# A decoder block's gate matrix, built by one-hot matmuls or scattered into cleared DRAM

## The chip, the cores and the metric

One core of one Trainium2 chip. The metric is the device time of one execution in microseconds (us), the median of the runs. The kernel before takes 4041.68 us (three runs, 4041.59 to 4042.62).

## The reference, cut to what matters

One layer of a decoder with 512 tokens and a model width of 2048: a linear recurrence and a latent attention side by side, a channel mixer called PEER, a gated embedding and a last norm. The change is in PEER:

```python
s1 = jnp.einsum('nhc,kc->nhk', q[:, :, 0], k1)      # 8 heads, 128 keys a half
s2 = jnp.einsum('nhc,kc->nhk', q[:, :, 1], k2)
v1, i1 = lax.top_k(s1, K)                           # K = 16
v2, i2 = lax.top_k(s2, K)
cand = (v1[..., :, None] + v2[..., None, :]).reshape(N, PEER_HEADS, K * K)
cv, ci = lax.top_k(cand, K)
e_idx = i1[ci // K] * 128 + i2[ci % K]              # 16384 experts
gate = softmax(cv)
z = einsum('thkd,td->thk', u_tab[e_idx], h)
out = einsum('thk,thkd->td', gelu(z) * gate, v_tab[e_idx])
```

Each token has 8 heads x 16 = 128 slots; a slot is an expert (a pair i1, i2 of 128 values each) and a gate. The 16 experts of one head differ; two heads can choose the same expert, and then their gates add up.

## The kernel before, in words

All matmuls run on float32 numbers split into a high and a low float32r part, three products each (`mm3`, L147 to L149). Weights come in blocks of 128x2048 by `Ahead` (L121 to L144): SyncE's queue (SP) loads a block two steps ahead into four half-block buffers, ScalarE (ACT) writes the high part (L111), VectorE (DVE) the low part (L112), one step ahead of TensorE (PE).

PEER treats its tokens in two groups. For group A (the first 128 tokens) GpSimd (POOL) gathers each token's expert rows by an indirect DMA, one slot of 128 tokens each (`gather`, L777); DVE multiplies a gathered row of `peer_u` with h and sums it (`dot_u`, L783 to L790) and then issues the gather that is two slots ahead, since there are two row buffers. Group B (the other 384 tokens) takes a dense path: all experts' z are computed for all tokens and multiplied with a gate matrix G over (i1, i2, token), which is zero where a token has not chosen the expert.

The U loop (L1010) has 128 steps, one per value j of i2: 48 matmuls of 384 columns give z for 128 experts and 384 tokens; ACT applies Gelu and stores it to `z_s` in DRAM (`finish`, L982). The V loop has 128 steps too: `act_load` (L991) brings z and G of four j back on SP's queue, `act_mul` (L1000) multiplies, `act_split` splits, and 48 matmuls of 384 columns follow. The first `act_load` stands in step 122 of the U loop, the first `act_mul` in step 124.

The top-k of group B's three blocks of 128 tokens (`topk`, `prep_B`) and the gate matrix are spread over the U loop's steps by a list of work with costs (L964 to L971): block 0's top-k in steps 7 to 23; then twice 36 steps with the next block's top-k and the gate matrices of the block before (a list of 32 quads of four tokens); and in the last 22 steps, up to step 117, block 2's quads. The gate matrix of a quad is made by `gate_tokens` (L821): per token ACT makes a one-hot row of i1 (L832, L838), DVE a one-hot row of i2 times the gate's two parts (L833), PE a matmul of 256 columns (L843); ACT and DVE write the result into `stage` (L848, L849), and every 32 tokens ACT's queue sends 2 MB to `G_s` (L851). Before that, `turn` (L801) transposes i1, i2 and the gates of a block (L807, L810). A hold keeps further work back for two steps around these.

The whole stretch from L871 on is under `tc.manual_schedule()`: every engine's instructions run in the order in which they are written. Earlier, `gate_proj` (L449), 32 times, multiplies x with the columns of the two branches' gates, while attention and the merge go on; each is one block of weights.

Of the kernel before, what the change touches and what calls it, by code (L numbers as in the profile page):

```python
# [10 lines left out]
F32 = mybir.dt.float32  # L11
F32R = mybir.dt.float32r
U32 = mybir.dt.uint32
# [20 lines left out]
def _pieces(value, count, bits):  # L34
    """value as a sum of `count` float32 numbers; all but the last have `bits` significant bits."""
    out, rest = [], value
    for _ in range(count - 1):
        m, e = math.frexp(rest)
        p = math.ldexp(math.floor(m * 2 ** bits), e - bits)
        out.append(p)  # L40
        rest -= p
    out.append(float(np.float32(rest)))
    return out
# [3 lines left out]
def kernel(ctx: ExitStack, tc: tile.TileContext, a, dbg=None):  # L47
# [14 lines left out]
    # ---------------------------------------------------------------- helpers  # L62
# [14 lines left out]
    class Ring:  # L77
        """Buffers taken in turn."""
# [14 lines left out]
    class Stream:  # L93
        """A [128, 2048] block of weights, loaded and split in two halves: part(i, n) is the i-th of n
        pieces as two float32r parts whose sum is exact."""
# [25 lines left out]
    class Ahead:  # L121
        """Streams of a list of blocks: loaded two steps ahead, split one step ahead."""
# [28 lines left out]
    def split(hi, lo, src, gain=None):  # L151
        """hi + lo = src * gain, both float32r."""
        if gain is None:
            S.activation(hi, src, AF.Copy)
            V.tensor_tensor(lo, src, hi.bitcast(F32), op=OP.subtract)  # L155
        else:
            S.activation(hi, src, AF.Copy, scale=gain)
            V.scalar_tensor_tensor(lo, src, gain, hi.bitcast(F32), op0=OP.mult, op1=OP.subtract)

    def cols_proj(src, xh, xl, kt=KT):  # L160
        """PSUM [128 output columns, T] for one column tile."""
# [6 lines left out]
    def rows_proj(srcs, blocks, before=None):  # L168
        """PSUM [128 tokens, 512 columns] for each token block."""
# [12 lines left out]
    def rstd_cols(ss, n, name):  # L182
        """[128 tokens, blocks] of 1/sqrt(ss/n + eps)."""
# [13 lines left out]
    def sums_over_features(sq):  # L197
        """[128 tokens, 4] PSUM sums over the partitions of sq [128, T]."""
# [6 lines left out]
    def rows_of(rc, out=None):  # L205
        """[128, tokens], in out or else in PSUM: every partition holds the row of rc."""
# [11 lines left out]
    class SumSq:  # L218
        """Sum of squares of [128, T] chunks over features."""
# [18 lines left out]
    # ---------------------------------------------------------------- constants  # L238
    masks = const.tile([128, 384], F32R, name="masks")
    cst = const.tile([128, 386], F32, name="cst")  # L240
    negmask, ident, iota = cst[:, :128], cst[:, 128:256], cst[:, 256:384]
    freq, sgn = cst[:, 384:385], cst[:, 385:386]
    tril = const.tile([128, 128], U32, name="tril")
# [16 lines left out]
    # ---------------------------------------------------------------- DRAM scratch  # L260
# [8 lines left out]
    G_s = dram.tile([NB // TC, 128, 128 * TC], F32, name="G_s")  # L269

    # ---------------------------------------------------------------- x * gain, split
# [28 lines left out]
    # ---------------------------------------------------------------- HGRN2  # L300
# [147 lines left out]
    # ---------------------------------------------------------------- gates (kept before the sigmoid)  # L448
    def gate_proj(src, dst):  # L449
        ps = cols_proj(src, xh, xl)  # L450
        t = t2()
        V.tensor_tensor(t, ps, rr_mix, op=OP.mult)
        nc.sync.dma_start(dst, t)

    # ---------------------------------------------------------------- MLA
# [17 lines left out]
    # rotary tables: angle = position * frequency, reduced to [-pi, pi]  # L473
# [49 lines left out]
    for hp in range(4):  # L523
# [21 lines left out]
        # a head's rotary part: its 64 rows of high parts, and in the other 64 rows their low parts  # L545
# [58 lines left out]
    # ---------------------------------------------------------------- merge  # L604
# [33 lines left out]
    opool.release()  # L638

    # ---------------------------------------------------------------- residual, second norm  # L640
# [45 lines left out]
    # ---------------------------------------------------------------- PEER top-k  # L686
    def topk16(*rows):
        """The 16 largest of each row (values, indices, row); the rows are overwritten."""
# [12 lines left out]
    def topk(b, i1o, i2o, gate):  # L701
        """Steps (cost, function) that fill i1o, i2o, gate: [128 tokens, 8 heads * 16] float32."""
# [57 lines left out]
    # ---- group A: expert rows gathered for the first 128 tokens  # L760
# [31 lines left out]
    # ---- group B: the gate matrix [i1, i2, token]  # L792
    slots = {}
    after_pe, after_pe_next, hold = [], [], [0]

    def prep_B(b):
        i1 = upool.tile([128, 128], F32, name="i1", bufs=2)
        i2 = upool.tile([128, 128], F32, name="i2", bufs=2)
        gt = upool.tile([128, 128], F32, name="gt", bufs=1)

        def turn():  # L801
            slots[b] = upool.tile([128, 4, 128], F32, name="slots", bufs=1)

            def pe():
                ps = mx()
                for n, t in enumerate((i1, i2, gt)):
                    TE.transpose(ps[:, n * 128:n * 128 + 128], t, ident)  # L807

                def act():
                    S.activation(flat(slots[b][:, :2]), ps[:, :256], AF.Copy)  # L810
                    split(slots[b][:, 2].bitcast(F32R), slots[b][:, 3], ps[:, 256:384])
                return act

            after_pe.append(lambda: after_pe_next.append(pe))
            hold[0] = 2

        return topk(b + 1, i1, i2, gt) + [(0, turn)]

    stage = [None]

    def gate_tokens(t0):  # L821
        """Gate matrices of tokens t0 .. t0+3 of group B."""
        if t0 % TC == 0:
            stage[0] = upool.tile([128, 128, TC], F32, name="stage", bufs=1)
        st = stage[0]
        hot = []
        for i in range(4):
            b, t = divmod(t0 + i, 128)
            l = upool.tile([128, 128], F32R, name="ohl", bufs=8)
            r = upool.tile([128, 2, 128], F32R, name="ohr", bufs=8)  # L830
            i1T, i2T = (slots[b][:, n, t:t + 1] for n in range(2))
            S.activation(l, iota, AF.Abs, scale=-1.0, bias=i1T)  # L832
            V.scalar_tensor_tensor(r, iota[:, None, :].to_broadcast([128, 2, 128]), i2T,  # L833
                                   slots[b][:, 2:4, t:t + 1].to_broadcast([128, 2, 128]),
                                   op0=OP.is_equal, op1=OP.mult)
            hot.append((l, r))
        for l, _ in hot:
            S.activation(l, l.bitcast(F32), AF.Relu, scale=-1.0, bias=ones[:, :1])  # L838

        def pe():  # L840
            ps = wide()
            for i, (l, r) in enumerate(hot):
                TE.matmul(ps[:, i * 256:i * 256 + 256], lhsT=l, rhs=flat(r), start=True, stop=True)  # L843

            def act():
                o = t0 % TC
                hi, lo = (ps.rearrange("p (t s j) -> p s j t", t=4, s=2)[:, n] for n in range(2))
                S.activation(st[:, :, o:o + 4], hi, AF.Copy)  # L848
                V.tensor_tensor(st[:, :, o:o + 4], st[:, :, o:o + 4], lo, op=OP.add)  # L849
                if o == TC - 4:  # L850
                    nc.scalar.dma_start(G_s[t0 // TC], flat(st))  # L851
            return act

        after_pe.append(pe)
        if t0 % TC == TC - 4:
            hold[0] = 2

    def merge(*lists):
        """The lists' steps in one list, each list spread evenly over it."""
# [3 lines left out]
    quads = [[(2, lambda t=t: gate_tokens(t)) for t in range(b * 128, (b + 1) * 128, 4)] for b in range(3)]  # L863

    def phase(steps, work):
        """The work with costs that sum to the steps of the loop it takes."""
# [3 lines left out]
    # ---------------------------------------------------------------- PEER scores  # L870
    ordered = tc.manual_schedule()  # L871
# [37 lines left out]
    def rows_of_h(c):  # L909
        """Group A's h by rows, 512 of its columns."""  # L910
# [10 lines left out]
    for cg in range(4):  # L921
# [28 lines left out]
        if cg == 0:  # L950
# [11 lines left out]
            # the top-k steps of group A that need the heads of a column group only  # L962
# [5 lines left out]
            for b in (1, 2):  # L968
                prep = prep_B(b)
                work += phase(MIX, merge(prep[:-1], quads[b - 1]) + prep[-1:])  # L970
# [20 lines left out]
    def act_load(grp, q):  # L991
# [3 lines left out]
        o = (grp * NJ + q * NQ) * TC  # L995
        nc.sync.dma_start(gt.rearrange("p t j i -> p t (j i)"),
                          G_s.rearrange("t p x -> p t x")[:, :, o:o + NQ * TC])
        parts_in[grp, q] = (zt, gt)

    def act_mul(grp, j):  # L1000
        zt, gt = parts_in[grp, j // NQ]
        zj = zt[:, j % NQ].rearrange("p (t i) -> p t i", i=TC)
        V.tensor_tensor(zj, zj, gt[:, :, j % NQ], op=OP.mult)
# [6 lines left out]
    for j in range(NU):  # L1010
# [6 lines left out]
        if j >= NF:  # L1017
            n = j + 1 - NF
            hold[0] = max(0, hold[0] - 1)
            while work and spent < n and not hold[0] and len(after_pe) < 2:  # L1020
# [13 lines left out]
        todo = after_pe + after_pe_next  # L1034
        after_pe.clear()
        after_pe_next.clear()
        for f in todo:
            g = f()
            if g:
                late.append(g)  # L1040
        if j == NU - 7:
            for f in late[1:]:
                f()
            late = late[:1]
# [4 lines left out]
            gts = Ring(vwA, 2, [128, NB // TC, 4, TC], F32, "gt")  # L1049
# [326 lines left out]
```

## Time and profile before

| what | value |
|---|---|
| median of three runs | 4041.68 us |
| the profiled execution: span from the first to the last instruction | 4040.0 us |
| what the profile shows around the span | nothing; the median is 1.7 us longer |
| PE busy | 4005.3 us (99%) |
| DVE busy | 2621.1 us (65%) |
| ACT busy | 1597.2 us (40%) |
| POOL busy | 347.6 us (9%) |
| DMA | 862.68 MB, mean 214 GB/s |
| granted TensorE clock | 0.998 |

The page gives busy times per engine and, in 40 slices of the span, each engine's busy tenths. A busy PE is not PE at its peak, since matmuls overlap: their starts, not their durations, give their pace. POOL's spans are rough. An idle engine that is not the bottleneck costs nothing.

### The profile page before, as it was taken

The numbers are of one execution on the slowest core, as the hardware profiler recorded it, in microseconds if no ns is written. First come the engines' busy times: TensorE is split into PE (matmuls) and PEld (weight loads), VectorE is DVE, ScalarE is ACT, GpSimd is POOL, SyncE is SP. The second block draws the span as 40 slices with busy tenths as digits, with TensorE's granted clock in tenths as the row PEclk, the third lists the DMA queues.
The fourth block names the chain that finished last, engine by engine and source line by source line (L and its number), as shares of the span: only waits on it lengthen the run. The fifth ranks groups of instructions, "written<-read, shape, count | busy, mean of one in ns | idle before, by whom it ended". The sixth has DMA issues, their size and how long they took to land. (4 is left out here: it accounts for less than half of the span.)

```text
span 4040.0 us, 54629 instructions
## 1 busy us (share of the span) xinstructions
PE 4005.3 (99%) x21191; PEld 3667.2 (91%) x21191; DVE 2621.1 (65%) x3992; ACT 1597.2 (40%) x2582; POOL 347.6 (9%) x262
## 2 busy tenths in 40 slices
PE   9999999999999999999999999999999999999998
PEld 7878777778888889999999999999999999999976
DVE  5352554443343343699998998977777888877744
ACT  5342433332332242325566555753333333333443
POOL 0000000000000000021221211111111111111000
PEclk9999999999999999999999999999999999999999
DMA  5222222334444442478787788789888888888432
GB/s 210 97 74 94 72 96 84 102 105 141 151 141 133 141 140 99 166 286 304 283 303 283 287 302 298 293 332 356 317 297 315 312 311 312 299 313 310 169 117 97
DMA packets 264515, 862.68 MB, mean 214 GB/s; under 512 B 24128, under 2 KB 94272, under 8 KB 229568
## 3 DMA queue, kind: packets, MB, share of 16 engines
q1 hardware_dynamic: 202064, 531.57, 38.5%
q0 software_dynamic: 36864, 268.45, 17.8%
q10 hardware_dynamic: 25328, 59.17, 3.8%
q8 instruction: 168, 2.75, 0.3%
q14 instruction: 91, 0.75, 0.1%
HBM read 780.44 MB, written 78.64 MB: 213 GB/s over the span
## 5 line engine op out<-in xcount | busy, mean ns | idle before, releaser
L111 ACT ACTIVATE hi<-raw 128x1024 fp32r<-128x1024 f32 x806 | 851.4, 1059 | 1606.9 <-PE acc L148 1371.9
L112 DVE TENSOR_TENSOR lo<-raw,hi 128x1024 fp32r<-128x1024 f32 x806 | 975.0, 1221 | 782.6 <-ACT hi L111 779.5
L147 PE MATMUL acc<-hBh,hi 128*128 128x384 f32 x2304 | 775.0, 336 | 0.0
L148 PE MATMUL acc<-hBl,hi 128*128 128x384 f32 x2304 | 774.5, 336 | 0.0
L149 PE MATMUL acc<-hBh,lo 128*128 128x384 f32 x2304 | 774.4, 336 | 0.0
L148 PEld LDWEIGHTS acc<-hBl,hi 128*128 128x128 f32 x2304 | 433.1, 188 | 3.0 <-DVE hBl L155 0.2
L147 PEld LDWEIGHTS acc<-hBh,hi 128*128 128x128 f32 x2304 | 433.1, 188 | 2.7
L149 PEld LDWEIGHTS acc<-hBh,lo 128*128 128x128 f32 x2304 | 433.1, 188 | 0.0
L779 POOL DMA_INDIRECT row<-in_peer_u_dram,eA x128 | 198.9, 1554 | 2551.1 <-DMA raw<-in_uT_dram 1703.2
L149 PE MATMUL acc<-xh,lo 128*128 128x512 f32 x912 | 363.9, 399 | 0.0
L147 PE MATMUL acc<-xh,hi 128*128 128x512 f32 x912 | 363.4, 398 | 0.0
L148 PE MATMUL acc<-xl,hi 128*128 128x512 f32 x912 | 362.6, 398 | 0.0
L147 PE MATMUL acc<-ahx,hi 128*128 128x384 f32 x1024 | 344.7, 337 | 0.0
L148 PE MATMUL acc<-alx,hi 128*128 128x384 f32 x1024 | 344.1, 336 | 0.0
L149 PE MATMUL acc<-ahx,lo 128*128 128x384 f32 x1024 | 344.1, 336 | 0.0
L147 PE MATMUL acc<-ah,hi 128*128 128x384 f32 x1024 | 344.1, 336 | 0.0
L148 PE MATMUL acc<-al,hi 128*128 128x384 f32 x1024 | 344.1, 336 | 0.0
L149 PE MATMUL acc<-ah,lo 128*128 128x384 f32 x1024 | 344.1, 336 | 0.0
L1083 DVE SCALAR_TENSOR_TENSOR outA<-row,coef,outA 128x2048 f32<-128x2048 f32 x127 | 298.0, 2346 | 16.6 <-DMA row<-in_peer_v_dram,eA 16.3
L785 DVE SCALAR_TENSOR_TENSOR row<-row,hrow 128x2048 f32<-128x2048 f32 x128 | 292.0, 2283 | 20.5 <-DMA row<-in_peer_u_dram,eA 20.4
L779 POOL DMA_INDIRECT row<-in_peer_v_dram,eA x128 | 147.5, 1152 | 860.3 <-DVE outA L1083 799.6
L149 PEld LDWEIGHTS acc<-xh,lo 128*128 128x128 f32 x912 | 171.4, 188 | 43.0 <-issue 2.4
(379 smaller groups left out, 6270.5 us busy)
## 6 DMA issues: line engine op xcount, KB each, us to landing
raw<-in_uT_dram SPq DMA_DIRECT2D x256, 512.0 KB, 6.9
raw<-in_vB_dram SPq DMA_DIRECT2D x256, 512.0 KB, 5.7
z_s<-t ACTq DMA_DIRECT2D x128, 192.0 KB, 4.9
G_s<-stage ACTq DMA_DIRECT2D x12, 2048.0 KB, 14.4
zt<-z_s SPq DMA_DIRECT2D x32, 768.0 KB, 7.4
gt<-G_s SPq DMA_DIRECT2D x32, 768.0 KB, 12.1
raw<-in_w_ga_dram SPq DMA_DIRECT2D x32, 512.0 KB, 3.5
raw<-in_w_gb_dram SPq DMA_DIRECT2D x32, 512.0 KB, 3.5
```

Source lines behind the costliest of these rows:

```text
L111: S.activation(hi, raw, AF.Copy)
L112: V.tensor_tensor(lo, raw, hi.bitcast(F32), op=OP.subtract)
L147: TE.matmul(out, lhsT=lh, rhs=rh, start=start, stop=False)
L148: TE.matmul(out, lhsT=lh, rhs=rl, start=False, stop=False)
L149: TE.matmul(out, lhsT=ll, rhs=rh, start=False, stop=stop)
L779: G.indirect_dma_start(out=row, out_offset=None, in_=tab, in_offset=bass.IndirectOffsetOnAxis(ap=eA[:, s:s + 1], axis=0))
L785: V.scalar_tensor_tensor(row, row, 1.0, hrow, op0=OP.mult, op1=OP.mult, accum_out=zA[:, s:s + 1])
L1083: V.scalar_tensor_tensor(outA, row, coef[:, s:s + 1], outA, op0=OP.mult, op1=OP.add)
```

## The change

The gate matrix `G_s` gets the order (i2, i1, token). It is cleared by 32 DMAs on ACT's queue, one per `gate_proj`, each writing four values of i2 (768 KB) from a tile of zeros. The one-hot rows, their matmuls, the stage and the transposes go. Instead, when a block's top-k is done, DVE works out for each token and slot the element's place in `G_s` (`places`, three instructions a block), and for each slot POOL issues one indirect DMA that adds the 128 tokens' gates to 128 elements of four bytes (`scatter`): 128 a block, 384 in all, four at a time in the places of the quads. The 16 scatters of a head are declared independent of each other; each waits for all of the head before. `act_load` reads runs of 1536 bytes where it read runs of 512. POOL is taken out of the hand-written order: the planner sets the order of its instructions when it compiles.

```diff
-    G_s = dram.tile([NB // TC, 128, 128 * TC], F32, name="G_s")
+    G_s = dram.tile([128, 128, NB], F32, name="G_s")
...
+    zpool = tc.alloc_tile_pool(name="zpool", bufs=1, side="left")
+    zeros = zpool.tile([128, NB], F32, name="zeros")
+    G.memset(zeros, 0.0)
+
+    def clear(j0):
+
+        nc.scalar.dma_start(G_s.rearrange("j i t -> i j t")[:, j0:j0 + 4], zeros[:, None, :].to_broadcast([128, 4, NB]))
+
     def gate_proj(src, dst):
+        clear(4 * (32 - len(gates_todo) - 1))
         ps = cols_proj(src, xh, xl)
...
-        return topk(b + 1, i1, i2, gt) + [(0, turn)]
...
-    def gate_tokens(t0):
...
+        gate_b[b] = upool.tile([128, 128], F32, name="gt", bufs=2)
+
+        def places():
+
+            off_b[b] = upool.tile([128, 128], U32, name="off", bufs=2)
+            V.scalar_tensor_tensor(i2, i2, 128.0, i1, op0=OP.mult, op1=OP.add)
+            V.tensor_scalar(i2, i2, float(NB), tcol[:, b:b + 1], op0=OP.mult, op1=OP.add)
+            V.tensor_copy(off_b[b], i2)
+
+        return topk(b + 1, i1, i2, gate_b[b]) + [(1, places)]
+
+    G_flat = G_s.rearrange("j i t -> (j i t)")[:, None]
+    SYNC = mybir.DependencyInfo(mybir.DependencyClass.Sync, mybir.DependencyReason.DATA)
+
+    def scatter(b, s):
+
+
+        ins = G.indirect_dma_start(out=G_flat, in_=gate_b[b][:, s:s + 1], in_offset=None,
+                                   out_offset=bass.IndirectOffsetOnAxis(ap=off_b[b][:, s:s + 1], axis=0),
+                                   compute_op=OP.add).ins
+        if s % 16 == 0:
+            before_head[b], this_head[b] = this_head.get(b, []), []
+        for other in this_head[b]:
+            tc.declare_no_dep(ins, other, reason="a head's experts differ")
+        for other in before_head[b]:
+            tc.add_manual_dep(ins, other.name, SYNC, reason="experts of two heads can be the same")
+        this_head[b].append(ins)
+
+    def gate_tokens(b, s0):
+        for s in range(s0, s0 + 4):
+            scatter(b, s)
...
-    quads = [[(2, lambda t=t: gate_tokens(t)) for t in range(b * 128, (b + 1) * 128, 4)] for b in range(3)]
+    quads = [[(2, lambda b=b, s=s: gate_tokens(b, s)) for s in range(0, 128, 4)] for b in range(3)]
...
-    ordered = tc.manual_schedule()
+    E = mybir.EngineType
+    ordered = tc.manual_schedule(engines={E.PE, E.DVE, E.Activation, E.SP})
...
-                work += phase(MIX, merge(prep[:-1], quads[b - 1]) + prep[-1:])
+                work += phase(MIX, merge(prep, quads[b - 1]))
...
-        o = (grp * NJ + q * NQ) * TC
-        nc.sync.dma_start(gt.rearrange("p t j i -> p t (j i)"),
-                          G_s.rearrange("t p x -> p t x")[:, :, o:o + NQ * TC])
+        j0 = grp * NJ + q * NQ
+        nc.sync.dma_start(gt, G_s.rearrange("j i t -> i j t")[:, j0:j0 + NQ])
...
-            hold[0] = max(0, hold[0] - 1)
-            while work and spent < n and not hold[0] and len(after_pe) < 2:
+            while work and spent < n:
```

## Rows read from the trace of the kernel before

**Rows 1.** The page: busy time, and the span in 40 slices.

```profile
PE 4005.3 (99%) x21191; PEld 3667.2 (91%) x21191; DVE 2621.1 (65%) x3992; ACT 1597.2 (40%) x2582; POOL 347.6 (9%) x262
...
DVE  5352554443343343699998998977777888877744
...
POOL 0000000000000000021221211111111111111000
PEclk9999999999999999999999999999999999999999
```

**Rows 2.** Busy time by stretch: gates and merge, U loop's last steps, V loop.

```profile
core 0: us, PE busy (x) PEld busy (x) DVE busy (x) ACT busy (x) POOL busy (x), PEclk, DMA share, GB/s
1040.00:1500.00 460.00, 459.07 (x2026) 376.54 (x2026) 191.33 (x241) 152.24 (x207) 0.00 (x0) 1.00 0.44 143
...
2160.00:2480.00 320.00, 314.42 (x1821) 309.92 (x1820) 286.41 (x537) 182.58 (x397) 56.06 (x36) 1.00 0.79 290
...
2800.00:3700.00 900.00, 900.00 (x5194) 900.00 (x5193) 718.12 (x765) 286.02 (x325) 132.27 (x115) 1.00 0.87 312
```

**Rows 3.** PE's timeline around one quad: start us, us, engine, line.

```profile
2127.28 0.34 PE L149 MATMUL acc<-hBh,lo 128*128 128x384 f32 x1
2127.45 0.63 PE L843 MATMUL wide<-ohr,ohl 128*128 128x256 f32 x4
2127.93 0.34 PE L147 MATMUL acc<-hBh,hi 128*128 128x384 f32 x1
2128.10 0.34 PE L148 MATMUL acc<-hBl,hi 128*128 128x384 f32 x1
...
2128.45 0.34 PE L147 MATMUL acc<-hBh,hi 128*128 128x384 f32 x1
```

**Rows 4.** PE's timeline around one turn's three transposes.

```profile
1844.73 0.38 PE L807 MATMUL wide<-cst,i 128*128 128x128 f32 x2
...
1844.97 0.42 PE L147 MATMUL acc<-hBh,hi 128*128 128x384 f32 x1
```

**Rows 5.** Groups of the U loop that the change removes: count, busy, mean, idle before.

```profile
L843 PE MATMUL wide<-ohr,ohl 128*128 128x256 f32 x384 | 62.5, 286 | 6.8 <-DVE ohr L833 5.1 <-ACT t L984 0.8
L833 DVE SCALAR_TENSOR_TENSOR ohr<-cst,slots 128x256 fp32r<-128x256 f32 x384 | 157.6, 477 | 0.1
L849 DVE TENSOR_TENSOR stage<-stage,wide 128x512 f32<-128x512 f32 x96 | 63.1, 682 | 5.6 <-ACT stage L848 5.2
```

**Rows 6.** The gathered rows, all instances: min, median, max, first and last start.

```profile
L779 POOL DMA_INDIRECT row<-in_peer_u_dram,eA x128: 934/1679/2747, 1704.9 to 2750.8; - x128
L785 DVE SCALAR_TENSOR_TENSOR row<-row,hrow x128: 2260/2283/2364, 1715.3 to 2758.8; 128x2048 f32<-128x2048 f32 x128
```

**Rows 7.** POOL's and DVE's timelines around two gathers.

```profile
2153.29 1.68 POOL L779 DMA_INDIRECT row<-in_peer_u_dram,eA  x1 [6.05 <-DVE row L785]
2159.04 0.94 POOL L779 DMA_INDIRECT row<-in_peer_u_dram,eA  x1 [4.07 <-DVE row L785]
...
2152.94 1.22 DVE L112 TENSOR_TENSOR lo<-raw,hi 128x1024 fp32r<-128x1024 f32 x1
...
2159.14 1.23 DVE L112 TENSOR_TENSOR lo<-raw,hi 128x1024 fp32r<-128x1024 f32 x1 [0.36 <-ACT hi L111]
```

**Rows 8.** The gathers of `peer_u` as one group: busy us, mean ns.

```profile
L779 POOL DMA_INDIRECT row<-in_peer_u_dram,eA x128 | 198.9, 1554 | 2551.1 <-DMA raw<-in_uT_dram 1703.2 <-DVE row L785 844.2 <-DVE lo L112 3.1
```

**Rows 9.** DMA issues: KB each, median us from issue to landing.

```profile
z_s<-t ACTq DMA_DIRECT2D x128, 192.0 KB, 4.9
G_s<-stage ACTq DMA_DIRECT2D x12, 2048.0 KB, 14.4
zt<-z_s SPq DMA_DIRECT2D x32, 768.0 KB, 7.4
gt<-G_s SPq DMA_DIRECT2D x32, 768.0 KB, 12.1
...
x1s<-x SPq DMA_DIRECT2D x16, 256.0 KB, 2.0
...
row<-in_peer_u_dram,eA POOLq DMA_INDIRECT x128, 9.0
```

**Rows 10.** ACT's timeline while gates are projected.

```profile
1048.18 1.06 ACT L111 ACTIVATE hi<-raw 128x1024 fp32r<-128x1024 f32 x1 [3.68 <-PE acc L148]
1053.79 1.06 ACT L111 ACTIVATE hi<-raw 128x1024 fp32r<-128x1024 f32 x1 [4.54 <-PE acc L148]
```

More of the change, by code (lines that the diff above doesn't have):

```diff
@@ L239 @@
     masks = const.tile([128, 384], F32R, name="masks")
-    cst = const.tile([128, 386], F32, name="cst")
+    cst = const.tile([128, 389], F32, name="cst")
     negmask, ident, iota = cst[:, :128], cst[:, 128:256], cst[:, 256:384]
     freq, sgn = cst[:, 384:385], cst[:, 385:386]
+    tcol = cst[:, 386:389]
     tril = const.tile([128, 128], U32, name="tril")
@@ L638 @@
     opool.release()
+    zpool.release()
     x1pool = tc.alloc_tile_pool(name="x1pool", bufs=1, side="left")
@@ L790, in dot_u @@
             gather(a["peer_v"], s + 2 - 128)
-    slots = {}
-    after_pe, after_pe_next, hold = [], [], [0]
+    off_b, gate_b = {}, {}
+    before_head, this_head = {}, {}
     def prep_B(b):
@@ L798, in prep_B @@
         i2 = upool.tile([128, 128], F32, name="i2", bufs=2)
[L799 to L815, printed above, removed]
@@ L817, in prep_B @@
-        return topk(b + 1, i1, i2, gt) + [(0, turn)]
-    stage = [None]
-    def gate_tokens(t0):
[L823 to L856, printed above, removed]
@@ L1001, in act_mul @@
         zt, gt = parts_in[grp, j // NQ]
-        zj = zt[:, j % NQ].rearrange("p (t i) -> p t i", i=TC)
-        V.tensor_tensor(zj, zj, gt[:, :, j % NQ], op=OP.mult)
+        zj = zt[:, j % NQ]
+        V.tensor_tensor(zj, zj, gt[:, j % NQ], op=OP.mult)
     def act_split(grp, j):
@@ L1033 @@
             scores_mul(3, pending)
[L1034 to L1040, printed above, removed]
         if j == NU - 7:
-            for f in late[1:]:
-                f()
-            late = late[:1]
             assert not work
@@ L1048 @@
             zts = Ring(vwA, 2, [128, 4, NB], F32, "zt")
-            gts = Ring(vwA, 2, [128, NB // TC, 4, TC], F32, "gt")
+            gts = Ring(vwA, 2, [128, 4, NB], F32, "gtl")
             vwB = tc.alloc_tile_pool(name="vwB", bufs=1, side="left")
@@ L1353, in _layout @@
         [neg, np.eye(128), np.broadcast_to(t[None, :], (128, 128)), fr[p % 32][:, None],
-         np.where(p < 32, -1.0, 1.0)[:, None]], axis=1).astype(np.float32)
+         np.where(p < 32, -1.0, 1.0)[:, None], t[:, None] + 128 * np.arange(3)], axis=1).astype(np.float32)
     return o
```

## The prediction

> **What bounds the kernel now.** I read the page first: PE is busy 99% of the span at the full granted clock, DVE 65%, POOL 9% [rows 1]. The reader should see that only work taken off PE shortens this kernel, or a wait that lets it run dry. DVE's slices 17 to 21 stand at 8 and 9 tenths [rows 1]: that is the start of the U loop, where top-k, dots and one-hot rows fall together. Next the busy times by stretch: in the V loop PE is busy 900 of 900 us with DMA at 0.87 and 312 GB/s; in the middle of the U loop it is busy 314.42 of 320 with DMA at 0.79 [rows 2]. So the DMA engines can carry the V loop's load without a stall, and the U loop loses a little to waits. The timeline gives the pace: 384-column matmuls start 0.173 us apart (three in 0.52 us, from 2127.93 to 2128.45), so a step of 48 lasts 8.32 us, and a quad's four matmuls, 2127.45 to 2127.93, cost 0.48 us [rows 3].
>
> **What leaves PE.** 96 quads x 0.48 = 46.1 us. A turn's three transposes take 0.24 us, 1844.73 to 1844.97 [rows 4]; three turns, 0.7. PE's idle time ahead of the quads' matmuls is 6.8 us, most of it waiting for DVE's one-hot rows [rows 5]; it goes too. Sum 53.6 us, all on the path. DVE loses 157.6 + 63.1 = 220.7 us [rows 5] and gains nine short instructions (`places`), which lie in that gap; nothing waits for DVE that did not before, so this is worth nothing beyond the 6.8.
>
> **What POOL gets.** 384 indirect DMAs with 128 offsets each. The trace has no scatter and no accumulating DMA; the nearest row is the gather, also 128 offsets: 0.934 us at least, 1.679 in the median, 2.747 at most [rows 6]. Two gathers of the timeline show why it has two levels: at 2153.29 DVE was in the middle of `lo` (2152.94 to 2154.16), and the gather took 1.68, ending 0.81 after it; at 2159.04 DVE was between instructions, and it took 0.94 although a `lo` began at 2159.14 [rows 7]. So POOL waits at its start for the DVE instruction under way. Scatters come at any time, DVE will be some two thirds busy, so I take the middle of the two levels, 1.31 us. Ends for the range: 0.94, and 2.75 if each waits for a long dot or has more to do than a gather.
>
> **The waits of the heads.** The first scatter of a head waits until the head before has landed; 24 waits, on POOL's queue, with the gathers behind. A store of 256 KB lands in 2.0 us in a quiet stretch, `z_s` with 192 KB in 4.9 us in this loop, a gather of 1 MB in 9.0 [rows 9]. I take 4.9, the loop's own smallest store; ends 2.0 and 9.0. The Trainium skill (DMA: Bandwidth & Descriptors, Anatomy of one DMA) puts the fixed part of such a DMA at about 2.0 us. By that the eight waits of a block would cost 16 us instead of 39, and the give-back worked out below would vanish; the row of this loop is more than twice as long, and no run here shows a small one from POOL.
>
> **Does POOL keep up?** A gather costs 1.554 in the mean [rows 8] and one falls every 8.24 us (127 intervals from 1704.9 to 2750.8 [rows 6]). Blocks 0 and 1 have 36 steps, 299.6 us: 128 x 1.31 + 8 x 4.9 + 36 x 1.55 = 262.7, it fits. Block 2 has 27 steps from its top-k's end (step 95) to the first `act_load` (step 122), 224.6 us: 128 x 1.31 + 8 x 4.9 + 27 x 1.55 = 248.8, that is 24.2 over. Two steps of slack, 16.6 us, stand behind it: the parts loaded in step 122 are multiplied in step 124. So 7.6 us are given back. A late scatter holds SP at `act_load`, and behind it the weight blocks; a late gather holds the dot, and behind it on DVE the next `lo`. A gather may be late by some 5 us: two row buffers give 2 x 8.24 = 16.5 from one dot's end to the next use, less the dot 2.3 [rows 6] and the landing 9.0 [rows 9].
>
> **The rest.** 32 clears of 768 KB (25 MB) move the zeros' traffic to the gates' stage, where DMA stands at 0.44 [rows 2]. ACT, which issues them, waits 3.7 to 4.5 us for PE before each half block there [rows 10], and that its `hi` waits for PE and not for a load shows that the blocks lie ready. I take nothing; without that cover a load behind a clear could be late by the 12.1 us of a 768 KB transfer [rows 9] now and then, so up to 10 us in all. The 12 stores of 2 MB leave the U loop, a relief for its DMAs. `act_load` gets longer runs: its 12.1 us should come near the 7.4 of `zt` [rows 9], hidden, since PE never waits in the V loop [rows 2].
>
> **Sum.** The profiled execution's span is 4040.0; the median lies 1.7 us above, and I carry that. 4041.7 - 53.6 + 7.6 = 3995.7, say 3996. The forecast's own range: nothing given back, 3988; or a scatter as long as the mean gather, 1.55, which puts block 2 at 279.4 us, 54.8 over, 38.2 given back, 4026.
>
> **Rivals.** First, on the other side, **the order on POOL**. Its instructions are no longer in the written order; the planner places them when it compiles, by its own reckoning. A block's scatters need only `places` and the head before, so they can all be packed right behind it, with a gather wherever the planner reckons its dot done. What stands ahead of a gather on the chip must then run first. It decides from about five scatters between two gathers: (8.24 - 1.55) / 1.31 = 5.1. If the planner takes a scatter for 0.94 us, as an undisturbed gather, it puts (8.24 - 0.94) / 0.94 = 7.8 between two. These take 7.8 x 1.31 + 1.55 = 11.8 us, and half a head's wait 2.4 if it does not reckon with it: 3.5 to 5.9 us late for each of 384 / 7.8 = 49 gathers, 172 to 289 us. Less 15 for the gathers' slack at three blocks' starts, less 53.6: 4145 to 4262. For it: the gathers' two levels show that POOL depends on DVE, which a plan can hardly know, and one block fits only just even when spread evenly. Against: a planner that reckons two microseconds for a scatter spreads them and leaves the gathers in front. Chance 0.27.
>
> Second, **the DMA engines**. 384 x 128 elements are 3072 small packets per engine, read and written back. The nearest row: 768 KB as 1536 runs of 512 bytes (`gt`) land in 12.1 us, as 128 runs of 6144 (`zt`) in 7.4 [rows 9]; 4.7 us for 88 more packets per engine are 0.053 us each. Reading and writing, 3072 x 0.106 = 326 us of each engine in the 94 steps (782 us) of the scatters, 0.42 on top of 0.79, less 0.07 or so for the stores that go: 1.14, so the stretch would be 14% longer, +109 - 53.6: 4097. Against it: that difference of landings holds more than the packets' own time. The Trainium skill (DMA: Bandwidth & Descriptors, § Bandwidth) gives about 10.5 ns a packet; by that it would be 65 us of each engine and no bound, and the page's rule on transfers under 64 KB (dominated by descriptors) would cost nothing here. Chance 0.11.
>
> Third, **no overlap**: the change does not do what it says, and each scatter waits for the one before, since all write one tensor. 384 x (1.31 + 4.9) = 2385 us of POOL for 782 us: 4041.7 - 53.6 + 1603 = 5591. Against: the diff declares them independent. Chance 0.04.
>
> Fourth, **a draw**: POOL late in block 2 alone, by a scatter of 1.7 us: 128 x 1.7 + 39.2 + 41.9 = 298.7, 74 over, 57 given back, 4045. Chance 0.11.
>
> **How the numbers follow.** The forecast has 0.45; the remaining 0.02 are scatters of 2.75 us, block 2 then 433 us and blocks 0 and 1 447 each, +487 - 53.6, about 4475. About 0.2%, 8 us, is what a measurement of this kernel can tell from no change: faster means under 4033.6, slower over 4049.8. Faster 0.45 (the forecast), same 0.10 (most of the draw), slower 0.45 (order, DMA, no overlap, long scatters, the draw's rest). The range must take in both sides: from 3986 (all 53.6 gained and a little more) to 4210, which leaves out the upper part of the first rival (0.12), the third and the last, and 0.02 below. The likeliest case's own range is 3988 to 4026.
>
> **What would show it.** Right: no matmul other than the 48 in a step, PE without idle time in the U loop, steps of 8.32 us; scatters on POOL of 0.9 to 1.7 us; POOL busy about 0.9 in the second half of the U loop; SP's `act_load` waiting little. Wrong: DVE's dots idle for a gather by hundreds of us (the order), scatters waiting for landings one by one (no overlap), weight blocks landing late with DMA at 0.95 or more (the engines), or scatters of 2 us and more.

## The result, and the profile after

The changed kernel takes 4474.17 us (median of four runs, 4469.25 to 4477.88), the kernel before 4041.64 on the same chip: ratio 1.1068, 95% interval 1.1052 to 1.1084. It is 10.7% slower, where 3996 us and a range of 3986 to 4210 had been given. The profiled execution has a span of 4467.0 us and took 4469.25.

The page answers to [rows 1]: busy times, then three of the rows of 40 slices (112 us each).

```profile
PE 4032.5 (90%) x20798; PEld 3687.5 (83%) x20798; DVE 2413.8 (54%) x3518; ACT 1321.2 (30%) x1712; POOL 979.3 (22%) x647
...
PE   9999999999999999954894589657999999999998
...
POOL 0000000000000001578248843774111111111000
PEclk9999999999999999977997799878999999999999
```

POOL shows three humps, one per block of group B, and wherever it stands at 7 or 8 tenths PE stands at 4 to 6 and its granted clock is down. The busy times by stretch show the same: the first hump, and for comparison the V loop.

```profile
core 0: us, PE busy (x) PEld busy (x) DVE busy (x) ACT busy (x) POOL busy (x), PEclk, DMA share, GB/s
...
1850.00:2100.00 250.00, 131.47 (x645) 127.96 (x643) 77.81 (x180) 33.93 (x42) 197.93 (x121) 0.77 0.53 118
...
3300.00:4100.00 800.00, 800.00 (x4617) 800.00 (x4616) 640.10 (x682) 253.34 (x288) 119.84 (x103) 1.00 0.86 309
```

In the hump POOL works 198 of 250 us, PE 131, and the DMA engines are at 0.53, far from full. The V loop is as before [rows 2]. Next the waits: who waited for what, us in total, how often, the longest.

```profile
PE acc L149 <- DVE lo L112: 406.8, 39, 31.5
...
DVE row L796 <- DMA row<-in_peer_u_dram,eA: 622.8, 51, 26.0
...
POOL G_s L827 <- DMA G_s<-gt,off: 41.9, 23, 4.3
```

A dot waits for its gathered row, 51 times and up to 26 us; `lo` stands behind it on DVE; PE waits for `lo`. The heads' waits for one another, which the prediction had feared, are 41.9 us in all. The timelines of POOL, DVE and PE around one such stall (start us, us, engine, line; in brackets the idle time before and what ended it):

```profile
1908.06 2.41 POOL L827 DMA_INDIRECT G_s<-gt,off  x1 [0.30 <-issue]
1910.77 1.98 POOL L827 DMA_INDIRECT G_s<-gt,off  x1 [0.30 <-issue]
1913.06 1.00 POOL L790 DMA_INDIRECT row<-in_peer_u_dram,eA  x1 [0.30 <-DVE val L703]
1916.90 1.56 POOL L827 DMA_INDIRECT G_s<-gt,off  x1 [2.85 <-DMA G_s<-gt,off]
1918.77 1.55 POOL L827 DMA_INDIRECT G_s<-gt,off  x1 [0.30 <-issue]
...
1942.09 1.54 POOL L827 DMA_INDIRECT G_s<-gt,off  x1 [0.30 <-issue]
1943.94 1.54 POOL L827 DMA_INDIRECT G_s<-gt,off  x1 [0.31 <-issue]
1945.78 1.01 POOL L790 DMA_INDIRECT row<-in_peer_u_dram,eA  x1 [0.30 <-issue]
```

```profile
1908.98 2.35 DVE L112 TENSOR_TENSOR lo<-raw,hi 128x1024 fp32r<-128x1024 f32 x2
...
1927.65 0.28 DVE L705 FIND_INDEX8 idx<-val,scores 128x8 uint32<-128x128 f32 x1
1951.14 2.29 DVE L796 SCALAR_TENSOR_TENSOR row<-row,hrow 128x2048 f32<-128x2048 f32 x1 [23.21 <-DMA row<-in_peer_u_dram,eA]
...
1953.36 2.35 DVE L112 TENSOR_TENSOR lo<-raw,hi 128x1024 fp32r<-128x1024 f32 x2
```

```profile
1954.63 0.69 PE L149 MATMUL acc<-hBh,lo 128*128 128x384 f32 x1 [19.95 <-DVE lo L112]
1955.12 0.52 PE L147 MATMUL acc<-hBh,hi 128*128 128x384 f32 x1
1955.44 0.52 PE L148 MATMUL acc<-hBl,hi 128*128 128x384 f32 x1
...
1959.53 0.34 PE L147 MATMUL acc<-hBh,hi 128*128 128x384 f32 x1
1959.70 0.34 PE L148 MATMUL acc<-hBl,hi 128*128 128x384 f32 x1
```

Between the gathers of 1913.06 and 1945.78 POOL issues fifteen scatters, mostly one every 1.85 us (1943.94 less 1942.09): 1.54 busy, and 0.30 before the next begins though the profile names nothing that it waits for. The gather, 33 us after the one before instead of some 8, lands, and the dot starts, at 1951.14; `lo` follows, and PE goes on after 20 us of nothing. Its matmuls then start 0.32 us apart (1955.12, 1955.44), the level of 1.2 GHz, and further on 0.17 apart (1959.53, 1959.70), that of 2.4 GHz, as before [rows 3]. So a stall seems to be paid twice: in idle time, and in slow matmuls behind it.

The scatters and gathers as groups (busy us, mean ns, idle before), and each one's minimum, median and maximum in ns with its first and last start, answer to [rows 6, 8]:

```profile
L827 POOL DMA_INDIRECT G_s<-gt,off x384 | 663.3, 1727 | 178.3 <-issue 133.1 <-DMA G_s<-gt,off 41.9 <-ACT hi L111 3.3
L790 POOL DMA_INDIRECT row<-in_peer_u_dram,eA x128 | 167.6, 1310 | 1697.7 <-DMA raw<-in_uT_dram 1232.7 <-DVE row L796 448.5 <-issue 15.6
```

```profile
L827 POOL DMA_INDIRECT G_s<-gt,off x384: 1541/1543/3462, 1838.2 to 3061.5; - x192
...
L790 POOL DMA_INDIRECT row<-in_peer_u_dram,eA x128: 936/1010/2744, 1704.9 to 3178.1; - x128
```

A scatter costs POOL 1.54 us at least, where the shortest gather costs 0.94, and 1.727 in the mean; with the 0.30 ahead of it, 2.03. From the first to the last gather of `peer_u` it is now 1473.2 us; before it was 1045.9 [rows 6].

POOL's order is another than the written one. Right behind each `places` come a block's 128 scatters, in 15, 15 and 17 groups with a gather (twice two) between them: 47 groups, 384 / 47 = 8.17 scatters each in the mean, up to 15 in one. Then 23 or 24 gathers follow with no scatter between.

### The profile page after: what moved, and what is told of

It reads as the page before. It is cut to its first block, busy times and chain, and to the rows that moved or that the text cites. A ratio compares the mean times of both kernels' runs of the same rounds, so it can differ in the third digit from the quotient of the medians.

```text
span 4467.0 us, 52540 instructions
## 1 busy us (share of the span) xinstructions
PE 4032.5 (90%) x20798; PEld 3687.5 (83%) x20798; DVE 2413.8 (54%) x3518; ACT 1321.2 (30%) x1712; POOL 979.3 (22%) x647
## 3 DMA queue, kind: packets, MB, share of 16 engines
q0 software_dynamic: 92160, 268.67, 20.4%
## 5 line engine op out<-in xcount | busy, mean ns | idle before, releaser
L149 PE MATMUL acc<-hBh,lo 128*128 128x384 f32 x2304 | 811.3, 352 | 406.8 <-DVE lo L112 406.8
L149 PEld LDWEIGHTS acc<-hBh,lo 128*128 128x128 f32 x2304 | 457.2, 198 | 419.3 <-DVE lo L112 419.3
L147 PE MATMUL acc<-hBh,hi 128*128 128x384 f32 x2304 | 803.2, 349 | 0.0
L148 PE MATMUL acc<-hBl,hi 128*128 128x384 f32 x2304 | 801.4, 348 | 0.0
L827 POOL DMA_INDIRECT G_s<-gt,off x384 | 663.3, 1727 | 178.3 <-issue 133.1
L796 DVE SCALAR_TENSOR_TENSOR row<-row,hrow 128x2048 f32<-128x2048 f32 x128 | 292.2, 2285 | 622.8 <-DMA row<-in_peer_u_dram,eA 622.8
L790 POOL DMA_INDIRECT row<-in_peer_u_dram,eA x128 | 167.6, 1310 | 1697.7 <-DMA raw<-in_uT_dram 1232.7
L147 PEld LDWEIGHTS acc<-hBh,hi 128*128 128x128 f32 x2304 | 457.2, 198 | 2.6
L148 PEld LDWEIGHTS acc<-hBl,hi 128*128 128x128 f32 x2304 | 455.2, 198 | 3.0 <-DVE hBl L155 0.2
## 6 DMA issues: line engine op xcount, KB each, us to landing
gtl<-G_s SPq DMA_DIRECT2D x32, 768.0 KB, 11.5
```

The lines of the kernel that those rows point to most:

```text
L147: TE.matmul(out, lhsT=lh, rhs=rh, start=start, stop=False)
L148: TE.matmul(out, lhsT=lh, rhs=rl, start=False, stop=False)
L149: TE.matmul(out, lhsT=ll, rhs=rh, start=False, stop=stop)
L790: G.indirect_dma_start(out=row, out_offset=None, in_=tab, in_offset=bass.IndirectOffsetOnAxis(ap=eA[:, s:s + 1], axis=0))
L796: V.scalar_tensor_tensor(row, row, 1.0, hrow, op0=OP.mult, op1=OP.mult, accum_out=zA[:, s:s + 1])
L827: ins = G.indirect_dma_start(out=G_flat, in_=gate_b[b][:, s:s + 1], in_offset=None, out_offset=bass.IndirectOffsetOnAxis(ap=off_b[b][:, s: ...
```

## The experiments

Theory: POOL, in order, has more work than its time in the U loop, because a scatter costs more than it was taken for, and the planner's order then bunches that work. Rivals: the clears or another part of the change; the DMA engines; the heads' waits.

**No scatters.** All the rest of the change stays.

```diff
     def gate_tokens(b, s0):
-        for s in range(s0, s0 + 4):
-            scatter(b, s)
+        pass
```

> The scatters are left out, so the gate matrix stays zero and group B's part of PEER is missing; the clears, the offsets and the longer runs stay. Prediction's step 'what leaves PE': 4041.7 - 53.6 = 3988 us. If the clears or the other small parts cost something that the trace hides, up to 4000. If less than 30 us is gained (4012 or more), the step was wrong.

Measured: 3980.70 us, ratio 0.9847 (0.9831 to 0.9864). Its page, and its gathers (minimum, median and maximum in ns, first and last start):

```profile
PE 3950.4 (99%) x20798; PEld 3618.2 (91%) x20798; DVE 2417.4 (61%) x3518; ACT 1321.2 (33%) x1712; POOL 334.6 (8%) x263
...
q0 software_dynamic: 36864, 268.45, 18.2%
```

```profile
L790 POOL DMA_INDIRECT row<-in_peer_u_dram,eA x128: 933/1677/2747, 1704.0 to 2688.9; - x128
```

So clears, layout, `places` and the new `act_load` cost nothing that can be seen, and the whole loss comes with the scatters. The two pages give an account of it. The spans differ by 4467.0 - 3978.0 = 489.0 us. PE's idle time is 4467.0 - 4032.5 = 434.5 against 3978.0 - 3950.4 = 27.6: 406.9 more, which is the wait for `lo`. The same 20798 matmuls are busy 4032.5 against 3950.4: 82.1 more, at the lower granted clock. 406.9 + 82.1 = 489.0. And all of it lies in the U loop: from the first to the last gather it is 984.9 us here and 1473.2 in the changed kernel, 488.3 more.

**POOL in the written order.** Each scatter is placed behind the gather written last before it, each gather behind the scatters since.

```diff
+        for other in since:
+            tc.add_manual_dep(ins, other.name, NOSYNC, reason="written order")
+        since.clear()
+        lastg[0] = ins
...
+        tc.add_manual_dep(ins, lastg[0].name, NOSYNC, reason="written order")
+        since.append(ins)
```

> POOL's instructions stand in the order in which they are written (a quad's 4 scatters, then the gathers of the step), all else as in the change. Theory 'order' (the planner packs some 8.5 scatters between two gathers in three bursts, and the gathers are late): at most 8 now stand between two gathers, mostly 4. What is left is POOL's amount of work at 1.73 + 0.30 us a scatter and 1.31 + 0.30 a gather: blocks 0 and 1 need 332 us for 300 each, block 2 318 for 225, less 17 of slack: 142 lost, 53.6 gained, about 4130 us. Rival 'DMA' (the small packets slow all transfers): the order changes nothing, 4474 us. Rival 'head waits' (POOL stands still until a head has landed): 4474 or more, since the gathers now stand behind the waits.

Measured: 4272.44 us, ratio 1.0570 (1.0553 to 1.0588); 202 us better than the planner's order, but some 140 worse than expected. Two lines of its waits:

```profile
DVE row L802 <- DMA row<-in_peer_u_dram,eA: 529.5, 84, 16.6
...
PE acc L149 <- DVE lo L112: 213.6, 45, 16.8
```

The longest wait of a dot falls from 26.0 to 16.6, but there are 84 instead of 51. The order is a cause and not the whole of it. The scatters' mean here is 1.854, so 2.15 with the 0.30: the two 36-step phases hold 3.56 of them a step, the last 22 steps 5.82, or 12.5 us a step for the scatters alone. The expectation had not reckoned with a dearer scatter in an even order, which is 384 x 0.124 = 48 of the 142 us, and it gave the last block's scatters 27 steps where the written order has 22. By the stores of `z_s`, one a step, the two phases run at 10.2 and 10.5 us a step and the last 22 steps at 14.1; without scatters a step lasts 8.32 in all three.

**Four scatters a step.** The chain of the run above stays; the work is respread so that top-k 2 ends early enough and each step, behind its dot and gather, gets at most four.

```diff
-            B0, MIX = 16, 36
+            B0, MIX = 14, 32
...
-                work += phase(MIX, merge(prep, quads[b - 1]))
-            work += phase(NW - NF - B0 - 2 * MIX, quads[2])
+                work += phase(MIX, prep)
...
+            for _ in range(min(4, len(ready))):
+                scatter(*ready.pop(0))
```

> Gathers first, then at most 4 scatters in each step, and the three blocks' top-k done earlier (steps 21, 53 and 85), so that the scatters lie evenly over 96 steps. Theory 'order' with the amount of work as the rest: a step's POOL work is 4 x 2.03 + 1.61 + 0.45 = 10.2 us for 8.32, 180 lost over 96 steps, up to 41 of it taken up by the steps before the first load of the gate matrix, 53.6 gained: 4127 to 4168 us. Rival 'DMA': 4474 as before. If it is at 4042 or under, POOL's amount of work does not bind at all and only the order did.

Measured: 4230.68 us, ratio 1.0473 (1.0452 to 1.0493); the run above is 42 slower. The amount of work alone costs more than expected. Its groups on POOL, and the scatters' first and last start:

```profile
L835 POOL DMA_INDIRECT G_s<-gt,off x384 | 720.1, 1875 | 145.7 <-issue 116.6 <-DMA G_s<-gt,off 29.1
L792 POOL DMA_INDIRECT row<-in_peer_u_dram,eA x128 | 185.2, 1447 | 1409.5 <-ACT hi L111 1233.2 <-DVE row L802 143.2 <-issue 28.6
```

```profile
L835 POOL DMA_INDIRECT G_s<-gt,off x384: 1542/1565/3660, 1829.1 to 2871.2; - x192
```

A step lasts (2871.2 - 1829.1) / 96 = 10.86 us. POOL's own work in one is 4 x (1.875 + 0.30) for the scatters, 128 / 120 x (1.447 + 0.30) for the gathers (128 dots fall into 120 steps) and 29.1 / 96 of a head's wait: 8.70 + 1.86 + 0.30 = 10.86. Here POOL's work sets the pace: ahead of the 102 gathers of that stretch it waits for a dot for 1.8 us in all. Without scatters a step is 984.9 / 127 x 128 / 120 = 8.27 us; 96 x (10.86 - 8.27) = 249; the spans of the two profiles differ by 4219.1 - 3978.0 = 241, the medians by 250. (With the 8.32 of the stores of `z_s` it would be 244.) So of the 493 us that the scatters cost in the changed kernel 202 go with the planner's order, 42 more when the work is spread evenly as well, and about 250 stay, as their amount on POOL.

**Written without adding**, in the planner's order (a single run).

```diff
-                                   out_offset=bass.IndirectOffsetOnAxis(ap=off_b[b][:, s:s + 1], axis=0),
-                                   compute_op=OP.add).ins
+                                   out_offset=bass.IndirectOffsetOnAxis(ap=off_b[b][:, s:s + 1], axis=0)).ins
```

> The scatters write instead of adding (gates of two heads that chose the same expert are not summed); the planner orders POOL as it likes. Theory 'the add is dear on POOL': a scatter at its shortest falls from 1.54 to the gather's 0.94 us, 384 x 0.6 = 230 us less, about 4245 us. Theory 'the scatter itself is dear': 1.54 stays, and the time stays near 4474. Rival 'DMA' with the reading back as the cost: POOL's 1.54 stays and the time falls.

Measured: 4282.01 us. Its scatters as a group, then minimum, median and maximum, then its software queue's packets, bytes and share:

```profile
L827 POOL DMA_INDIRECT G_s<-gt,off x384 | 472.2, 1230 | 178.2 <-issue 138.1 <-DMA G_s<-gt,off 36.7 <-ACT hi L111 3.3
```

```profile
L827 POOL DMA_INDIRECT G_s<-gt,off x384: 954/959/2976, 1836.6 to 2873.2; - x192
```

```profile
q0 software_dynamic: 49152, 268.67, 17.3%
```

A plain scatter costs what a gather costs, 0.95 us; adding makes it 1.54. The gap of 0.30 and the heads' waits stay. 384 x (1.727 - 1.230) = 191 us, and the runs differ by 4474.17 - 4282.01 = 192: in the planner's order POOL's time goes into the kernel's one for one. The scatters stand in the same 47 groups as before. They also make fewer packets here; that POOL's time alone makes up the 192 us speaks against these as the cause, but the two were not separated. The saving was expected somewhat larger, by the undisturbed difference of 0.6 a scatter; but the shorter one is held longer by DVE: its mean lies 1.230 - 0.954 = 0.28 over its minimum, the adding one's 1.727 - 1.541 = 0.19.

**Four a step, without adding**: both edits together.

```diff
+            for _ in range(min(4, len(ready))):
+                scatter(*ready.pop(0))
...
-                                   compute_op=OP.add).ins
```

> As e4 (gathers first, four scatters a step), but the scatters write instead of adding, so gates of two heads that chose the same expert are not summed. Theory 'POOL's amount of work' (an adding scatter holds POOL for 1.54 us and more, a writing one for 0.95): a step now asks 4 x (1.23 + 0.30) + 1.45 + 0.30 + 0.3 = 8.2 us of POOL for 8.32, so POOL no longer binds and the time falls to that without scatters or a little over, 3981 to 4005 us. Rival 'the order still': about e4's 4231 less a small part, 4150 or more. Rival 'DMA': the packets of the plain write slow the loads, 4100 or more.

Measured: 4081.72 us, ratio 1.0090 (1.0074 to 1.0105): better than with adding by 149, and still slower than before, which I had not expected.

```profile
L835 POOL DMA_INDIRECT G_s<-gt,off x384 | 543.0, 1414 | 168.4 <-issue 125.5 <-DMA G_s<-gt,off 37.3 <-ACT hi L111 5.2
```

The expectation took the 1.23 of the planner's order; spread evenly the same scatter takes 1.41, as the adding one goes from 1.73 to 1.88. It then meets DVE at work more often. In the planner's order DVE stands still for much of a burst (it is busy 77.81 of the 250 us of the first hump), which makes the scatters cheap. A step of POOL is 4 x (1.414 + 0.30) + 128 / 120 x (1.449 + 0.30) + 37.3 / 96 = 9.1 us, over 8.27; the scatters' own starts give 9.41. The 0.3 between are further waits of POOL in that stretch: 51.8 us ahead of 105 gathers, where 0.30 each would be 31.5 (16.7 of them are for a dot), and 125.5 "issue" ahead of the scatters, where 0.30 each would be 115.2.

**Two blocks scattered, the third by one-hot matmuls**, two or three scatters a step in the chained order, from the kernel before; and **one block scattered, two by one-hot matmuls**, one or two a step. The one-hot blocks have a DRAM tile of their own; the scattered part keeps the old layout and is cleared. The diff shows the second; the first has `NS = 2` and `3 if j % 3 else 2`, and its top-k are moved accordingly.

```diff
+NS = 1
...
+    G_s = dram.tile([NT, 128, 128 * TC], F32, name="G_s")
+    G_o = dram.tile([NB // TC - NT, 128, 128 * TC], F32, name="G_o")
...
+            work = phase(B0, prep_S(0)) + phase(MIX, prep_B(1))
+            prep = prep_B(2)
+            work += phase(MIX, merge(prep[:-1], quads[1]) + prep[-1:])
...
+            for _ in range(min(1 + j % 2, len(ready))):
+                scatter(*ready.pop(0))
```

> The kernel before with two of the three blocks scattered (adding, gathers first, 2 or 3 scatters a step over 96 steps) and the third left to the one-hot matmuls. Theory 'POOL's amount': a step asks 2.67 x 2.18 + 1.75 + 0.2 = 7.8 us of POOL for 8.32 to 8.8, so POOL keeps up, and two thirds of the 62 us are gained: 3995 to 4010 us. Rival 'any scatter delays the gathers': two thirds of the loss, 4160 or more. If POOL's 7.8 is too near 8.3 because DVE holds it more often than in e4: 4010 to 4060.

> As e5 with one block scattered, 1 or 2 scatters a step, two blocks by one-hot matmuls. Theory 'POOL's amount': POOL has half of each step to spare, a third of the 62 us is gained: 4018 to 4026 us. Rival 'any scatter delays the gathers': 4060 or more.

Measured: two blocks 4036.32 us, ratio 0.9987 (0.9978 to 0.9996); one block **4022.11**, ratio 0.9952 (0.9939 to 0.9966). The second beats both kernels, by half a per cent. The dots' wait with two blocks, then the dots' and PE's with one:

```profile
DVE row L806 <- DMA row<-in_peer_u_dram,eA: 187.3, 58, 10.6
```

```profile
DVE row L806 <- DMA row<-in_peer_u_dram,eA: 27.0, 13, 7.0
...
PE wide L896 <- DVE ohr L886: 3.3, 3, 2.1
```

With one block the dots wait 27 us in all, never longer than 7.0, and PE, in the U loop, only those few us for one-hot rows; the gain, 4042.06 - 4022.11 = 20 us as expected, is a third of the 62 that go when the whole one-hot path goes. With two blocks a step of three scatters, two steps in three, is 3 x (1.944 + 0.30) + 128 / 120 x (1.544 + 0.30) = 8.7 us of POOL, and the mean step, with 44.8 / 96 for the heads' waits, is 8.4, again over 8.27: the dots wait 187 us, and the gain is smaller than with one, where the theory had expected more.

The dots' wait does not tell where these us are lost. By the stores of `z_s`, with two blocks, steps 23 to 95 last 8.43 and 8.50 us, hardly more than 8.32 without scatters; steps 95 to 117, in which the third block's one-hot rows are made, last 10.2, against 9.04 in the kernel before and with one block. That is 22 x 1.16 = 26 us, most of what is missing. PE's waits with two blocks:

```profile
PE wide L896 <- DVE ohr L886: 16.4, 2, 9.3
...
PE acc L150 <- DVE lo L113: 7.6, 6, 2.7
```

Both long waits fall into those steps: DVE waits for a late row, and the dot, `lo` and only then the one-hot rows follow. The clock granted there is lower too, 0.95 over these 22 steps.

## Why the prediction was wrong, point by point

**What leaves PE: right, mis-sized.** 53.6 us were given, 62 came (4042.74 - 3980.70, the runs of that chip). By the two pages PE's idle time falls by 34.7 - 27.6 = 7.1, close to the 6.8 reckoned, and its busy time by 4005.3 - 3950.4 = 54.9, where 46.1 + 0.7 had been reckoned. So the term that was too small is a quad's price: the one of [rows 3] was undisturbed. From the first matmul of a quad to the next of another kind, the 96 quads of the kernel before take 54.1 us, 0.56 each and not 0.48. Part of that is waiting which the quads' MATMUL row [rows 5] does not show as idle time; the row of their weight loads, which stand ahead of the matmuls on PE, has 12.1 us (groups of PE in the U and V loops):

```profile
L843 PEld LDWEIGHTS wide<-ohr,ohl 128*128 128x128 f32 x384 | 55.2, 188 | 12.1 <-ACT t L984 4.3 <-issue 3.6 <-ACT hi L111 3.3
```

With 12.1 in place of 6.8 the sum would be 58.9; the 3 us that are then left are not placed.

**What POOL gets: the step that failed.** "Scatters come at any time, DVE will be some two thirds busy, so I take the middle of the two levels, 1.31 us." That took a scatter for a gather. Measured: 1.54 undisturbed, 1.727 in the mean, and 0.30 before each: 2.03 instead of 1.31. That adding is dearer no row of before could show, and there the sum went by the nearest relative. The 0.30 one row did show, and I had not read it: the first two gathers of before follow each other at once on POOL, 0.30 apart with nothing to wait for.

```profile
1704.89 2.15 POOL L779 DMA_INDIRECT row<-in_peer_u_dram,eA  x1 [1703.16 <-DMA raw<-in_uT_dram]
1707.34 0.93 POOL L779 DMA_INDIRECT row<-in_peer_u_dram,eA  x1 [0.30 <-issue]
```

A busy time is not yet the price of an instruction; the distance between two starts is, and 384 x 0.30 = 115 us of POOL stood in that bracket. By the prediction's own sum blocks 0 and 1 then need 128 x 2.03 + 8 x 1.8 + 36 x 1.61 = 332 us for 299.6, and block 2 128 x 2.03 + 8 x 1.8 + 27 x 1.61 = 318 for 224.6: "it fits" falls for every block, and no order could have hidden the scatters in these steps. 384 x 0.72 = 276 us of POOL were missing in the sum; together the three blocks ask 332 + 332 + 318 = 982 us where the steps give 824, and the run with four a step, evenly spread, still loses about 250. The end of 2.75 had a chance of 0.02; its 4475 is close to the result by accident, since the median scatter took 1.54.

**The order on POOL: the right rival with too small a price.** It foresaw 7.8 scatters between two gathers and 49 late gathers; there are 8.17 and 47, and its sign came: dots idle for a gather, 622.8 us. That the planner takes a scatter for an undisturbed gather, from which the 7.8 came, was a guess, and no run shows what it reckons with. The rival priced a gap at 7.8 x 1.31 + 1.55 + 2.4 = 14.2 us at most. Measured terms give 8.17 x 2.03 + 1.61 + 0.9 = 19.1 (0.9 is half a head's wait of 1.8), less the 7.76 from gather to gather without scatters, times 47: 533. Less the same 15 for the gathers' slack, 518, against 488 measured. The mechanism had 0.27, the forecast's spread order 0.45: the wrong way round. The diff says that POOL leaves the hand-written order, and what a planner does with work that waits for nothing was the question to weigh most. Why it packs so many can't be read from a profile.

**The waits of the heads: too dear.** 41.9 us over 23 waits are 1.8 each, not 4.9. I took the loop's smallest store as nearest; the 2.0 us that the Trainium skill (DMA: Bandwidth & Descriptors, Anatomy of one DMA) gives for the fixed part of a DMA was nearer. The wait of 1.8 is close to it; a scatter's whole way from issue to landing is not, with 3.4 in the median, 1.54 of which pass on POOL before a wait can begin. This error went the other way and was small: 24 x 3.1 = 74 us too much.

**The DMA engines: rejected rightly, for a reason that was half wrong.** In the bursts their share is 0.53, and weight blocks of `uT` land in 4.8 us where they took 6.9 before; and the run with four a step makes the same packets and is 243 us faster. The price per packet came out close: by the software queue's rows of the changed kernel and of the run without scatters,

```profile
q0 software_dynamic: 92160, 268.67, 20.4%
```

0.204 x 4467.0 - 0.182 x 3978.0 = 187 us of each engine for (92160 - 36864) / 16 = 3456 packets, 0.054 us each (0.053 was estimated). That is luck. The estimate laid the 4.7 us between `gt` and `zt` to 88 more packets an engine, but in the changed kernel the runs of `gt` are three times as long, 64 packets an engine fewer, and it lands hardly sooner, in 11.5 us instead of 12.1, and not near `zt`'s 7.4 as the prediction also had it:

```profile
gtl<-G_s SPq DMA_DIRECT2D x32, 768.0 KB, 11.5
```

The Trainium skill (DMA: Bandwidth & Descriptors, § Bandwidth) gives about 10.5 ns a packet, a whole DMA's time over its 64 packets. The prediction read it as one engine's time for one of its own packets, which the Trainium skill does not say there, so the 0.054 us of this trace neither bear it out nor contradict it. The number of packets was too high: 55296 / 384 = 144 a scatter, not 256.

**The rest, no overlap, the draw.** The clears, `act_load` and `places` cost nothing, as taken (no scatters: 3981). Scatters of a head do follow each other at once (1.85 us apart), so the third rival falls. "A gather may be late by some 5 us" holds in kind: with one block, POOL's short delays cost PE nothing.

**What is shown and what is argued.** Shown by runs: the loss belongs to the scatters; half of it goes when they stand in a set order and are spread evenly; writing in place of adding saves 0.5 us each in time that counts (the planner's order by a single run). Read from waits and timelines: the chain scatter, gather, dot, `lo`, PE. Argued only: that the 82 us of slower matmuls follow from the idle stretches (the granted clock is 1.00 in the V loop, where PE is busy throughout, and 0.77 in the first hump, where it works 131 of 250 us). Not tried: taking the heads' waits away, for two heads' equal experts would then race.

## What to carry to other kernels

An engine that is 9% busy is no free place for hundreds of small instructions if a waited-for chain runs through its queue: work out its load per step with the instruction's price and the gap between two, and leave room, as one or two scatters a step did and four did not. Before an engine is taken out of a hand-written order, ask what a planner may put ahead of the instruction that others wait for. And a new kind of instruction (here an indirect DMA that adds) should be measured by itself before a sum rests on its nearest relative.

## What the runs showed of the hardware

- An indirect DMA of 128 four-byte elements costs POOL 0.95 us when it writes and 1.54 when it adds (minima of 384 each), and makes 32 packets or 144: (49152 - 36864) / 384 and (92160 - 36864) / 384. 144 is 128 + 16, as if adding had a packet of its own for each element.
- Between two indirect DMAs on POOL lie 0.30 us at least, even back to back with nothing to wait for; 384 of them are 115 us.
- Like a gather, a scatter waits at its start for the DVE instruction under way: that of 1910.77 took 1.98 us and ended 1.42 after the end of `lo` (1908.98 and 2.35 make 1911.33); a gather ended 0.81 after [rows 7]. So the same scatter is mostly dearer where DVE is busier: 1.727 in the mean with DVE busy 0.43 of the stretch of the scatters, 1.875 with 0.54 (four a step), 1.944 with 0.74 (two blocks). The share alone does not settle it: with one block DVE is busy 0.84 and the mean is 1.893.
